# YOCO decoder trunk: the first mixer's input products of two chunks by Strassen's scheme, and half of the gained weights split at first use

## The chip, the cores and the metric

The kernel runs on one core of a Trainium2 chip. The metric is the device time of one execution in microseconds (us); lower is better. Three runs of the kernel before took 1886.28, 1886.26 and 1881.32 us, so its median is 1886.26 us.

## The reference, cut to what matters

One sequence of 2048 positions, width 1024, 8 heads of 64, everything in fp32:

```python
h = rmsnorm(x, norm_a)
b, c, xin, g = split(h @ w_in_a, 4)             # (2048 x 1024) @ (1024 x 4096)
y = b * causal_conv3(c * xin, conv_a)           # depthwise, along the positions
x = x + (y * silu(g)) @ w_out_a
k, v = split(rmsnorm(x, norm_kv) @ w_kv, 2)     # computed once
h = rmsnorm(x, norm_b)
q, g = split(h @ w_in_b, 2)
o = stick_breaking_attention(q, k, v)           # strictly causal, no softmax
x = x + (o * silu(g)) @ w_out_b
out = rmsnorm(x, norm_f)
```

The change concerns `h @ w_in_a` for half of the positions, and the way in which `w_kv` and `w_in_b`, times their gains, are made ready for the later products.

## The kernel before

**Tiles.** Positions lie in 4 chunks of 512 columns; chunk 0 holds the last ones. The width is 8 blocks of 128 partitions. A product in fp32 is made from rounded halves: every operand is split into a high part (a cast on ScalarE, ACT) and a low part (a subtraction on VectorE, DVE; `split`, L174), and `mm3` (L203) runs high·high, high·low and low·high for each of the 8 contraction blocks: 24 matmuls of 128x512 into one PSUM bank, a "group". TensorE is PE below, GpSimd POOL, SyncE SP.

**The first mixer.** `mixer_in((0, 1))` (L284) is called m01 here. It runs over 8 channel blocks `cb`, the two chunks `c` and the four gates C, X, B, G: 64 groups. x of the two chunks is loaded once; it is multiplied by the gain `norm_a` only and split to `h` (L238, L239), so that products can start before the mean square of a position is known. Its reciprocal root, broadcast over partitions (`rs`, and `rs2`, its square, L250), is multiplied into the gates' results later (L331, L348, L350). The weights of each gate and block are loaded raw, split (`load_w`, L184) and stored split to DRAM for the chunks 2 and 3, which load them split.

**Beside it.** `stats_x` (L260) computes the mean squares of chunks 2 and 3, and `fold_gains` (L359) makes 16 blocks of w_kv and w_in_b ready: load in two halves, multiply by the gain (L368), split, store.

**Order.** The generators yield amounts of PE work, and `merge`, `take` and `run` interleave them by weights (L729 to L751): first a quarter of m01 alone, then the rest of it beside `stats_x` and `fold_gains`. After it come the out-projection of chunk 0 (`proj_out`, L376; `yr` is the mixer's y read back, `po` its product) and its k, q, v, then attention of the chunks, merged with the projections of others. The order on each engine is fixed when the program is built. An engine runs its instructions strictly in order, and SP starts nearly all DMAs, also in order, each after the semaphores that it waits for.

**Homes.** Tiles share named sets of buffers: a tile gets its buffer when the last reader of the tile that had it is done. m01's banks are `lin`, `z` and `wt`, two of each, in turn. Split weights are `whl`, 4 buffers of 8 KB a partition, raw ones `wraw`, 2 buffers. x lies in `w`, `R` and `ld`, the folds and `x1` in `og`.

## Time and profile before

| | us | share of the span |
|---|---|---|
| median of three runs | 1886.26 | |
| the profiled execution | 1879.31 | |
| its span, first to last instruction | 1877.6 | 100% |
| PE busy | 1771.9 | 94% |
| DVE busy | 1261.9 | 67% |
| ACT busy | 772.7 | 41% |
| POOL busy | 450.4 | 24% |
| the 16 DMA engines, on average, by the queue that SP and others feed | | 63.0% |

1.7 us of the profiled execution lie outside of its span, and it is 6.95 us shorter than the median. A busy PE is one that has a matmul in its pipeline; the granted clock, a share of full speed, says how fast it runs, and averages 0.979. The chain of waits is the work that ended last, followed back step by step to what released it; an instruction's idle time is the time that its engine stood still ahead of it, and the arrow after it names what ended that.

### The profile page before, as it was taken

The page shows a single profiled execution, that of the slowest core. Times are in us where ns is not written, and L with a number is a line of the kernel's source. Part 1 is how long each engine was busy: PE and PEld are TensorE (multiplying, and loading weights), DVE is VectorE, ACT ScalarE, POOL GpSimd, SP SyncE. Part 2 cuts the span into 40 slices and gives each one's busy share as a digit, 9 for nine tenths or more (in the row PEclk, how much of TensorE's full clock was granted, in tenths as well). Part 3 has the DMA queues.
Part 4 walks back from the last instruction along what each step waited for, and adds up shares of the span by engine and source line. Part 5 has one row for each costly group of instructions (what it writes and reads, how often), then busy time and mean ns, then how long its engine had stood idle before and what let it go on. Part 6 is the DMA issues. An engine that isn't in the chain of part 4 may idle for free.

```text
span 1877.6 us, 24951 instructions
## 1 busy us (share of the span) xinstructions
PE 1771.9 (94%) x8312; PEld 1447.6 (77%) x8312; DVE 1261.9 (67%) x1927; ACT 772.7 (41%) x1497; POOL 450.4 (24%) x822
## 2 busy tenths in 40 slices
PE   7999999999999999999999999999988998988783
PEld 5888888888778878887888888888766886866562
DVE  7876534554243364478785478787858889889984
ACT  6423212231232143345443244454535556556642
POOL 5100000101111032132221122232223214547543
PEclk9999999999999999999999999999999999999896
DMA  9999865697978798867677766566586667778763
GB/s 292 309 324 332 307 195 165 209 328 280 336 250 281 227 330 257 290 207 250 216 253 244 248 195 204 183 215 198 180 300 196 223 194 265 260 238 278 225 196 130
DMA packets 238480, 460.44 MB, mean 245 GB/s; under 512 B 18448, under 2 KB 133136, under 8 KB 213776
## 3 DMA queue, kind: packets, MB, share of 16 engines
q1 hardware_dynamic: 178272, 400.09, 63.0%
q10 hardware_dynamic: 59920, 58.74, 10.9%
q8 instruction: 66, 1.08, 0.2%
q14 instruction: 62, 0.51, 0.1%
q0 software_dynamic: 160, 0.02, 0.1%
HBM read 322.73 MB, written 136.05 MB: 244 GB/s over the span
## 4 chain that ended last, share of the span: by engine, by line
PE 74%; DVE 10%; DMA 7%; issue 4%; ACT 2%; POOL 2%; SPq 0%; ACTq 0%; POOLq 0%; DVEq 0%
PE pX L209 9%; PE pB L209 9%; PE po L209 9%; PE pG L209 9%; PE pC L209 8%; PE wt L526 4%; PE pv L209 4%; PE pk L209 3%; PE pq L209 3%; DVE R L514 3%; PE pg L209 3%; PE av L536 3%; PE av L535 2%; PE z L500 2%; PE z L501 2%
## 5 line engine op out<-in xcount | busy, mean ns | idle before, releaser
L514 DVE TENSOR_TENSOR_SCAN R<-R,R,ones 128x512 f32<-128x512 f32 x192 | 255.0, 1330 | 25.2 <-ACT R L503 24.7
L503 ACT ACTIVATE R<-z 128x512 f32<-128x512 f32 (+1 forms) x320 | 174.0, 544 | 185.0 <-PE z L501 72.7
L176 DVE TENSOR_TENSOR wtl<-wt,wth 128x512 fp32r<-128x512 f32 (+1 forms) x320 | 186.2, 601 | 79.9 <-ACT wth L175 76.8
L175 ACT CAST wth<-wt 128x512 fp32r<-128x512 f32 (+1 forms) x320 | 159.6, 528 | 184.7 <-PE wt L526 150.3
L518 DVE TENSOR_TENSOR w<-w,R 128x512 f32<-128x512 f32 (+1 forms) x320 | 207.7, 658 | 19.6 <-POOL R L511 2.1
L209 PE MATMUL pC<-h,whl_C 128*128 128x512 f32 x768 | 189.8, 396 | 11.0 <-ACT whl_C L175 8.0
L513 POOL COPY R<-R 128x1 f32<-128x1 f32 x192 | 117.4, 613 | 340.9 <-DVE R L514 308.6
L209 PE MATMUL po<-y,whl_o 128*128 128x512 f32 x768 | 189.2, 393 | 2.4 <-DVE x L394 2.0
L209 PE MATMUL pX<-h,whl_X 128*128 128x512 f32 x768 | 186.3, 392 | 1.3 <-DVE cv L354 1.3
L209 PE MATMUL pB<-h,whl_B 128*128 128x512 f32 x768 | 185.9, 392 | 0.0
L209 PE MATMUL pG<-h,whl_G 128*128 128x512 f32 x768 | 185.7, 392 | 0.0
L526 PE MATMUL wt<-ident,w 128*128 128x128 f32 x1088 | 176.8, 278 | 7.5 <-DVE w L518 4.5
L209 PEld LDWEIGHTS pC<-h,whl_C 128*128 128x128 f32 x768 | 143.5, 189 | 44.1 <-ACT whl_C L175 8.0
L505 ACT ACTIVATE w<-z 128x512 f32<-128x512 f32 (+1 forms) x320 | 172.1, 543 | 2.5 <-PE wt L526 2.4
L209 PEld LDWEIGHTS pX<-h,whl_X 128*128 128x128 f32 x768 | 143.5, 188 | 31.5 <-DVE cv L354 1.5
L209 PEld LDWEIGHTS po<-y,whl_o 128*128 128x128 f32 x768 | 142.7, 188 | 32.1 <-DVE x L394 2.2
L209 PEld LDWEIGHTS pB<-h,whl_B 128*128 128x128 f32 x768 | 143.5, 188 | 29.7
L209 PEld LDWEIGHTS pG<-h,whl_G 128*128 128x128 f32 x768 | 143.6, 188 | 29.5
L526 PEld LDWEIGHTS wt<-ident,w 128*128 128x128 f32 x1088 | 137.4, 143 | 36.0 <-DVE w L518 6.9
L536 PE MATMUL av<-wtl,vv 128*128 128x512 f32 (+1 forms) x320 | 127.3, 401 | 27.0 <-DVE wtl L176 26.5
L514 DVE TENSOR_TENSOR_SCAN R<-R,ones 128x512 f32<-128x512 f32 (+3 forms) x128 | 116.4, 915 | 37.0 <-POOL R L509 32.8
L500 PE MATMUL z<-kt,q 128*128 128x512 f32 (+1 forms) x320 | 129.3, 406 | 5.7 <-ACT w L505 2.8
(172 smaller groups left out, 2685.1 us busy)
## 6 DMA issues: line engine op xcount, KB each, us to landing
whl_o<-sw_o SPq DMA_DIRECT2D x24, 1024.0 KB, 5.3
kt<-k_d ACTq DMA_DIRECT2D x80, 256.0 KB, 4.0
vv<-v_d ACTq DMA_DIRECT2D x80, 256.0 KB, 3.7
whl_C<-sw_C SPq DMA_DIRECT2D x16, 1024.0 KB, 5.9
whl_X<-sw_X SPq DMA_DIRECT2D x16, 1024.0 KB, 5.3
whl_B<-sw_B SPq DMA_DIRECT2D x16, 1024.0 KB, 5.8
whl_G<-sw_G SPq DMA_DIRECT2D x16, 1024.0 KB, 5.3
whl_k<-sw_kv SPq DMA_DIRECT2D x16, 1024.0 KB, 7.0
```

Source lines behind the costliest of these rows:

```text
L175: nc.scalar.copy(hi, src)
L176: eng.tensor_sub(lo, src, hi.bitcast(F32))
L209: ins = nc.tensor.matmul(ps, w[:, k, :], a[k][:, m, :], start=n == 0, stop=n == 3 * kt - 1)
L500: nc.tensor.matmul(ps[:, lom:CH], q2[:, 0, qi * P:(qi + 1) * P], kt[:, lom:CH], start=True, stop=False)
L501: nc.tensor.matmul(ps[:, lom:CH], q2[:, 1, qi * P:(qi + 1) * P], kt[:, lom:CH], start=False, stop=True)
L503: nc.scalar.activation(R[:, lo + 1:CH + 1], ps[:, lo:CH], AF.Sigmoid, scale=-0.125)
L505: nc.scalar.activation(w[:, lo:CH], ps[:, lo:CH], AF.Sigmoid, scale=0.125)
L513: nc.gpsimd.tensor_copy(R[:, 0:1], carry[qi])
L514: nc.vector.tensor_tensor_scan(out=R[:, lo + 1:CH + 1], data0=R[:, lo + 1:CH + 1], data1=ones[:, 0:1].to_broadcast([P, CH - lo]), initial= ...
L518: nc.vector.tensor_mul(w[:, lo:CH], w[:, lo:CH], R[:, lo:CH])
L526: nc.tensor.transpose(wt[:, qi * P:(qi + 1) * P], ws[qi][:, kb * P:(kb + 1) * P], ident)
L536: ins = nc.tensor.matmul(av[:, 0:n], vs, wl[:, 0:n], start=False, stop=final)
```

## The change

**Strassen's scheme.** For channel blocks 2 to 7 of m01 two gates (C and X, or B and G) and the two chunks form a 2x2 block product over the two halves of the contraction (k blocks 0 to 3 and 4 to 7): rows are the gates, columns the chunks. Winograd's form needs 7 products of half length in place of 8. Such a unit has 7 x 4 x 3 = 84 matmuls in place of 96, and there are 12 units. The operands are sums. On the weights' side, for every unit (`fast_weights`): a11, a21, a22, a12 and s1 to s4, from 4 raw tiles, 8 splits, two DVE and two POOL additions. On the x side, once (`fast_operands`, called at the second channel block, and `fast_rest`, at the start of the fast part): x of both chunks is scaled by gain and reciprocal root in 16 DVE instructions, 16 POOL subtractions make the sums, and 28 tiles are split: b11, t1, t2, b22, b21, t3, t4, 4 tiles each. The results are put together by `keep` (ACT copies out of PSUM, 4 a unit) and 3 DVE additions. Since x is scaled, the multiplications by `rs` and `rs2` go there.

**First use.** `fold_gains` makes 8 of its 16 blocks in m01. The other 8 (k and q blocks 2 and 3, g blocks 0 to 3) are loaded raw, multiplied and split by `load_w` where they are first used, in `proj_rest(0)` and in the gate projection of chunk 2.

**Halves.** Split weights are held, loaded and stored in halves of 4 k blocks (256 and 512 KB a DMA in place of 512 and 1024), everywhere.

**Smaller edits.** The gate of the two chunks uses Silu in place of Sigmoid and a product; x and the bank of sums have other homes; loads of `stats_x` and `fold_gains` are held behind PE's progress (`follow`); chunk 0's last y stays in SBUF (`y_last`); the weights of `merge` and `take` change.

```diff
-NR, NW, NT, NL, NWB, NRAW, NA, NWTS = 5, 8, 4, 5, 4, 2, 16, 2
+NR, NW, NT, NL, NWB, NRAW, NA, NWTS = 5, 8, 4, 5, 8, 4, 16, 2
...
+NPL = 2
+Q = 4
...
+    def load_w(src, key, nm, kt=KD, eng=nc.vector, gain=None):
+        first = key not in split_d
+        if first:
             split_d[key] = dram.tile([P, 2, kt, P], F32, name=f"sw_{nm}")
-            nc.sync.dma_start(out=split_d[key], in_=wt.bitcast(F32))
-            return wt
-        wt = w_tile(nm, kt)
-        nc.sync.dma_start(out=wt.bitcast(F32), in_=split_d[key])
-        return wt
+        wts = []
+        for j in range(0, kt, Q):
+            wt = w_tile(f"{nm}_{j}")
+            if first:
+                raw = sb.tile([P, Q, P], F32, name=f"wr_{nm}_{j}", tag="wraw", bufs=NRAW)
+                nc.sync.dma_start(out=raw, in_=src[j * P:(j + Q) * P, :].rearrange("(k p) n -> p k n", p=P))
+                if gain is not None:
+                    nc.vector.tensor_mul(raw, raw, gain[:, j:j + Q].unsqueeze(2).to_broadcast([P, Q, P]))
+                split(wt[:, 0], wt[:, 1], raw, eng)
+                nc.sync.dma_start(out=split_d[key][:, :, j:j + Q, :], in_=wt.bitcast(F32))
+            else:
+                nc.sync.dma_start(out=wt.bitcast(F32), in_=split_d[key][:, :, j:j + Q, :])
+            wts.append(wt)
+        return wts
...
-            tag, bufs = (("w", NW), ("R", NR) if k < NR else ("ld", NL))[c]
+            tag, bufs = (("og", KD), ("ld", NL) if k < NL else ("vv", 2) if k == NL else ("ot", 2))[c]
...
+            x = sb.tile([P, CH], F32, name=f"xs_{c}_{k}", tag="og", bufs=KD)
+            follow(nc.sync.dma_start(out=x, in_=xT[k * P:(k + 1) * P, cols(c)]))
...
-        for cb in range(KD):
+        for cb in range(KD if len(cs) == 1 else NPL):
             wts = {}
+            if cb == NPL - 1 and len(cs) > 1:
+                fast_operands()
...
-                    nc.scalar.activation(sg, sg, AF.Sigmoid)
-                    nc.vector.tensor_mul(t, t, late[c][1])
+                    nc.scalar.activation(sg, sg, AF.Silu)
+                    nc.vector.tensor_mul(t, t, late[c][0])
                 else:
                     nc.scalar.activation(sg, pG, AF.Sigmoid)
                 nc.vector.tensor_mul(t, t, sg)
-                nc.vector.tensor_mul(t, t, pG)
+                if c not in late:
+                    nc.vector.tensor_mul(t, t, pG)
                 nc.sync.dma_start(out=y_d[c][cb], in_=t)
                 yield rest(24)
...
+        if len(cs) > 1:
+            yield from mixer_fast()
...
+    def fast_operands():
+        x0, x1 = x_in[1], x_in[0]
+        for k in range(Q):
+            for c, x in ((1, x0), (0, x1)):
+                nc.vector.scalar_tensor_tensor(out=x[k], in0=x[k], scalar=gains["a"][:, k:k + 1], in1=late[c][0],
+                                               op0=ALU.mult, op1=ALU.mult)
+        w2 = ("w", NW)
+        operand("b11", x0[:Q], [(w2, w2)] * Q)
+        for k in range(Q):
+            nc.gpsimd.tensor_sub(x0[k], x1[k], x0[k])
+        hs = [("R", NR)] * 5 + [("wth", NWTS)] * 2 + [("wtl", NWTS)]
+        operand("t1", x0[:Q], [(hs[2 * k], hs[2 * k + 1]) for k in range(Q)])
+        for k in range(Q):
+            for c, x in ((0, x1), (1, x0)):
+                nc.vector.scalar_tensor_tensor(out=x[k + Q], in0=x[k + Q], scalar=gains["a"][:, k + Q:k + Q + 1],
+                                               in1=late[c][0], op0=ALU.mult, op1=ALU.mult)
+            nc.gpsimd.tensor_sub(x0[k], x1[k + Q], x0[k])
+            nc.gpsimd.tensor_sub(x1[k], x1[k + Q], x1[k])
+    def fast_rest():
+        x0, x1 = x_in[1], x_in[0]
+        act = ["act"] * Q
+        operand("t2", x0[:Q], act)
+        operand("b22", x1[Q:], act)
+        operand("b21", x0[Q:], act)
+        operand("t3", x1[:Q], act)
+        for k in range(Q):
+            nc.gpsimd.tensor_sub(x0[k + Q], x0[k + Q], x0[k])
+        operand("t4", x0[Q:], ["q2", "q2", (("kt", 2), ("kt", 2)), (("vv", 2), ("vv", 2))])
+    def fast_weights(n, cb, gs):
+        nm = f"{gs[0][0]}{cb}"
+        if n % 2 == 0:
+            raws = [sb.tile([P, Q, P], F32, name=f"fr_{nm}_{i}", tag="wraw", bufs=NRAW) for i in range(4)]
+        else:
+            pair = sb.tile([P, 2, Q, P], F32, name=f"fr_{nm}", tag="hl", bufs=1)
+            raws = [pair[:, 0], pair[:, 1]] + [sb.tile([P, Q, P], F32, name=f"fr_{nm}_{i}", tag="ot", bufs=2) for i in range(2)]
+        a11, a12, a21, a22 = raws
+        w = {}
+        def sp(key, raw):
+            w[key] = w_tile(f"{key}_{nm}")
+            split(w[key][:, 0], w[key][:, 1], raw)
+        for key, raw, (g, i), j in (("a11", a11, gs[0], 0), ("a21", a21, gs[1], 0), ("a22", a22, gs[1], Q), ("a12", a12, gs[0], Q)):
+            src = w_in_a[0][j * P:(j + Q) * P, i * D + cb * P: i * D + (cb + 1) * P]
+            nc.sync.dma_start(out=raw, in_=src.rearrange("(k p) n -> p k n", p=P))
+        for key, raw, (g, i), j in (("a11", a11, gs[0], 0), ("a21", a21, gs[1], 0), ("a22", a22, gs[1], Q), ("a12", a12, gs[0], Q)):
+            sp(key, raw)
+            if (g, cb) not in split_d:
+                split_d[g, cb] = dram.tile([P, 2, KD, P], F32, name=f"sw_{g}{cb}")
+            nc.sync.dma_start(out=split_d[g, cb][:, :, j:j + Q, :], in_=w[key].bitcast(F32))
+            if key == "a22":
+                nc.vector.tensor_add(a22, a21, a22)
+                sp("s1", a22)
+                nc.gpsimd.tensor_sub(a21, a11, a21)
+                nc.vector.tensor_sub(a11, a22, a11)
+                sp("s2", a11)
+        nc.gpsimd.tensor_sub(a12, a12, a11)
+        sp("s4", a12)
+        sp("s3", a21)
+        return w
...
+        def product(bank, w, b, start, stop):
+            n = 0
+            for k in range(Q):
+                for i, m in ((0, 0), (0, 1), (1, 0)):
+                    beat[:] = [nc.tensor.matmul(bank, w[:, i, k, :], ops[b][k][m], start=start and n == 0,
+                                                stop=stop and n == 3 * Q - 1, skip_group_check=True)]
+                    n += 1
+            return 3 * Q * MM
...
+        def keep(nm, ps):
+            t = ld512(nm)
+            nc.scalar.copy(t, ps)
+            return t
...
+        def out_of(cb, c, b, g):
+            t = conv[cb, c]
+            nc.vector.tensor_mul(t, t, b)
+            sg = t512(f"sg_{cb}_{c}")
+            nc.scalar.activation(sg, g, AF.Silu)
+            nc.vector.tensor_mul(t, t, sg)
+            if c == 0 and cb == KD - 1:
+                y_last.append(act_tile("y_0", cb))
+                split(y_last[0][:, 0, :], y_last[0][:, 1, :], t)
+            else:
+                nc.sync.dma_start(out=y_d[c][cb], in_=t)
...
+        for n, (cb, gs) in enumerate(units):
+            nm = f"{gs[0][0]}{cb}"
+            w = ws.pop(n)
+            a = bank(f"fa_{nm}", "lin", NLIN)
+            d = bank(f"fd_{nm}", "z", NZ)
+            c = bank(f"fc_{nm}", "wt", NWT)
+            yield product(a, w["a11"], "b11", True, False)
+            c0 = keep(f"f1_{nm}", a)
+            yield product(d, w["s1"], "t1", True, False)
+            p5 = keep(f"f5_{nm}", d)
+            final = n == len(units) - 1
+            if not final:
+                ws[n + 1] = fast_weights(n + 1, *units[n + 1])
+            if prev:
+                yield last_product(n - 1)
+            yield product(a, w["s2"], "t2", False, False)
+            c1 = keep(f"f2_{nm}", a)
+            yield product(d, w["s4"], "b22", False, True)
+            nc.vector.tensor_add(c1, c1, d)
+            if not final:
+                yield product(c, w["a12"], "b21", True, True)
+                nc.vector.tensor_add(c0, c0, c)
+            yield product(a, w["s3"], "t3", False, False)
+            x1 = keep(f"f3_{nm}", a)
+            nc.vector.tensor_add(x1, x1, p5)
+            if final:
+                yield product(c, w["a12"], "b21", True, True)
+                nc.vector.tensor_add(c0, c0, c)
+            if n % 2 == 0:
+                conv[cb] = conv_of(cb, 0, x1, c1)
+            else:
+                out_of(cb, 0, c1, x1)
+            prev.append((cb, gs, w, a, c0, c1, x1))
+        yield last_product(len(units) - 1)
...
+    def fold_gains(blocks):
...
+    def load_kv(i, nm):
+        return load_w(w_kv[:, i * P:(i + 1) * P], ("kv", i), nm, gain=gains["kv"])
...
+            if c == 0 and k == KD - 1:
+                y.append(y_last[0])
+                continue
             y.append(act_tile(f"y_{c}", k))
-            t = ld512(f"yr_{c}_{k}")
+            t = sb.tile([P, CH], F32, name=f"yr_{c}_{k}", tag="og", bufs=KD) if c == 0 else ld512(f"yr_{c}_{k}")
...
-        wts = load_w(None, ("kv", kb), f"k{c}_{kb}")
+        wts = load_kv(kb, f"k{c}_{kb}")
...
-    run(take(m01, TA / 4))
-    merge((m01, 1.75 * TA), (chain(iter((DLY,)), stats_x(2), stats_x(3), fold_gains()), 18.0 + DLY))
+    run(take(m01, TA / 2))
+    merge((m01, 1.3 * TA), (chain(iter((DLY,)), stats_x(2), stats_x(3), fold_gains([("kv", 0), ("b", 0), ("kv", 4), ("kv", 1), ("b", 1), ("kv", 5), ("kv", 6), ("kv", 7)])), 10.0 + DLY))
```

The rows below give the order on an engine in the program: line, operation, tile written, tiles read. A name ends in block, chunk and a running number, which differs between the two programs.

First DVE, where the fast part begins. `op_` tiles are the x side's operands (their raws are `xh_chunk_block`), `whl_` the weight side's, of unit C2 (block 2, gates C and X) and B2 (B and G); `sg` and `cv` are the end of the block before, of the old scheme.

```order
L177 TENSOR_TENSOR op_b21_3_1128<-xh_1_7_560,op_b21_3_1128 128x512
L177 TENSOR_TENSOR whl_s3_C2_1200<-fr_C2_2_1163,whl_s3_C2_1200 128x512
L177 TENSOR_TENSOR op_t3_0_1131<-xh_0_0_251,op_t3_0_1131 128x512
L177 TENSOR_TENSOR op_t4_0_1147<-xh_1_4_545,op_t4_0_1147 128x512
L369 TENSOR_TENSOR sg_1_1_1089<-pG_1_1_1064,rs_1_704 128x512
L177 TENSOR_TENSOR op_t3_1_1134<-xh_0_1_269,op_t3_1_1134 128x512
L177 TENSOR_TENSOR op_t3_2_1137<-xh_0_2_274,op_t3_2_1137 128x512
L177 TENSOR_TENSOR op_t4_1_1150<-xh_1_5_550,op_t4_1_1150 128x512
L177 TENSOR_TENSOR op_t3_3_1140<-xh_0_3_279,op_t3_3_1140 128x512
L177 TENSOR_TENSOR whl_a11_B2_1241<-fr_B2_1234,whl_a11_B2_1241 128x512
L177 TENSOR_TENSOR op_t4_2_1_1154<-xh_1_6_555,op_t4_2_0_1153 128x512
L374 TENSOR_TENSOR cv_1_1_1059<-cv_1_1_1059,sg_1_1_1089 128x512
```

Before, the same place of the program reads so; `whl_G2` is a full block of weights, `fold1_kv4` a fold.

```order
L348 TENSOR_TENSOR sg_1_1_984<-pG_1_1_959,rs_1_681 128x512
L368 TENSOR_TENSOR fold1_kv4_4_1753<-fold1_kv4_4_1753,g_kv_77 128x512
L176 TENSOR_TENSOR whl_G2_0_1217<-wr_G2_0_1218,whl_G2_0_1217 128x1024
L353 TENSOR_TENSOR cv_1_1_954<-cv_1_1_954,sg_1_1_984 128x512
L176 TENSOR_TENSOR fold1_kv4_4_1753<-fold1_kv4_4_1753,fold0_kv4_4_1752 128x512
L354 TENSOR_TENSOR cv_1_1_954<-cv_1_1_954,pG_1_1_959 128x512
```

The instruction that reads the last bank of the old scheme (`sg_1_1`) now stands behind the b21 splits and among those of t3 and t4, where folds and a weight stood.

PE at the start of the fast part, in the program of the change: `fc_C2` is the third product of the first unit, `fa_B2` the first of the second unit, `fa_C2` goes on with the first unit.

```order
L483 MATMUL fc_C2_1205<-op_b21_0_1119,whl_a12_C2_1192 128x512 x3
L483 MATMUL fc_C2_1205<-op_b21_1_1122,whl_a12_C2_1192 128x512 x3
L483 MATMUL fc_C2_1205<-op_b21_2_1125,whl_a12_C2_1192 128x512 x3
L483 MATMUL fc_C2_1205<-op_b21_3_1128,whl_a12_C2_1192 128x512 x3
L483 MATMUL fa_B2_1332<-op_b11_0_0_755,whl_a11_B2_1241 128x512
L483 MATMUL fa_B2_1332<-op_b11_0_1_756,whl_a11_B2_1241 128x512
L483 MATMUL fa_C2_1203<-op_t2_0_1095,whl_s2_C2_1189 128x512 x3
```

Before, that place holds the eight rows of `pC_2_0`, x3 each, that follow `pG_1_1`; their operands had been ready since the first block. Two matmuls of the second unit now stand ahead of the first unit's t2 product; `fa_B2` takes a `lin` bank.

ACT at the end of m01, in the program of the change: `y_0` are the casts that make chunk 0's y ready for `proj_out`, `sg_7_1` the gate from the last product of m01 (`fa_B7`).

```order
L493 COPY f3_B7_3207<-fa_B7_3094 128x512
L176 CAST whl_o0_2_4_3443<-wr_o0_2_4_3444 128x512
L176 CAST whl_o0_3_0_3482<-wr_o0_3_0_3483 128x512
L518 ACTIVATE sg_7_0_3224<-f3_B7_3207 128x512
L518 ACTIVATE sg_7_1_3243<-fa_B7_3094 128x512
L176 CAST whl_o0_3_4_3488<-wr_o0_3_4_3489 128x512
L176 CAST y_0_7_3227<-cv_7_0_3158 128x512
L176 CAST y_0_0_3247<-yr_0_0_3248 128x512
L176 CAST y_0_1_3252<-yr_0_1_3253 128x512
```

Before, on ACT at the end of m01:

```order
L175 CAST y_0_5_3002<-yr_0_5_3003 128x512
L175 CAST y_0_6_3007<-yr_0_6_3008 128x512
L349 ACTIVATE sg_7_0_2834<-sg_7_0_2834 128x512
L318 COPY cs_7_1_2866<-pC_7_1_2841 128x512
L175 CAST whl_o0_0_3018<-wr_o0_0_3019 128x1024
L175 CAST y_0_7_3012<-yr_0_7_3013 128x512
```

Seven of the eight y casts stood ahead of the gate of the last block; all of them now stand behind `sg_7_1`.

More of the change, by code (lines that the diff above doesn't have):

```diff
@@ L203, in mm3 @@
     def mm3(ps, wts, a, kt=KD):
-        hi, lo = wts[:, 0], wts[:, 1]
         n = 0
         for k in range(kt):
-            for w, m in ((hi, 0), (hi, 1), (lo, 0)):
-                ins = nc.tensor.matmul(ps, w[:, k, :], a[k][:, m, :], start=n == 0, stop=n == 3 * kt - 1)
+            for w, m in ((0, 0), (0, 1), (1, 0)):
+                ins = nc.tensor.matmul(ps, wts[k // Q][:, w, k % Q, :], a[k][:, m, :], start=n == 0, stop=n == 3 * kt - 1)
                 if fine[1] and len(anchors) > SLACK and n % GRP == 0:
@@ L281 @@
     turn = [0]
-    late_acc, late = {}, {}
+    late_acc, late, x_in = {}, {}, {}
     def mixer_in(cs):
@@ new lines, in fold_gains @@
+    def fold_gains(blocks):
+        for nm, i in blocks:
+            src, gain = (w_kv, gains["kv"]) if nm == "kv" else (w_in_b[0], gains["b"])
+            split_d[nm, i] = dram.tile([P, 2, KD, P], F32, name=f"sw_{nm}{i}")
+            for j in range(0, KD, Q):
+                hi, lo = (sb.tile([P, Q, P], F32R, name=f"fold{m}_{nm}{i}_{j}", tag="og", bufs=KD) for m in range(2))
+                raw = lo.bitcast(F32)
+                follow(nc.sync.dma_start(out=raw, in_=src[j * P:(j + Q) * P, i * P:(i + 1) * P].rearrange("(k p) n -> p k n", p=P)))
+                nc.vector.tensor_mul(raw, raw, gain[:, j:j + Q].unsqueeze(2).to_broadcast([P, Q, P]))
+                split(hi, lo, raw)
+                for m, t in enumerate((hi, lo)):
+                    nc.sync.dma_start(out=split_d[nm, i][:, m, j:j + Q, :], in_=t.bitcast(F32))
+            yield 1.0
```

102 lines of the change are left out of this document (70 added, 32 removed).

## Prediction

> **What bounds the kernel now.** I read the table of stages first (busy time of each engine, its count of instructions, granted clock, share of the DMA engines, GB/s). The second and third row below are the part in which m01 runs with full order.
>
> ```profile
> core 0: us, PE busy (x) PEld busy (x) DVE busy (x) ACT busy (x) POOL busy (x), PEclk, DMA share, GB/s
> 62.20:106.20 44.00, 44.00 (x195) 36.45 (x194) 30.67 (x46) 15.73 (x24) 2.46 (x5) 1.00 0.88 305
> 106.20:369.30 263.10, 263.10 (x1170) 218.28 (x1169) 141.05 (x212) 65.72 (x91) 12.80 (x27) 1.00 0.75 250
> 369.30:560.00 190.70, 185.60 (x831) 152.55 (x830) 82.22 (x145) 48.38 (x91) 19.24 (x49) 0.98 0.86 298
> 1000.00:1400.00 400.00, 394.05 (x1929) 325.28 (x1927) 291.26 (x422) 181.98 (x374) 97.48 (x201) 0.99 0.65 217
> ```
>
> Between 106.2 and 369.3 PE is never idle, at full clock, and DVE is busy for 141.05 of 263.10 us (54%). Nothing but the count of matmuls sets this stage. The chain of waits says the same of the whole, and PE's timeline (start, duration, and in brackets the idle time before) gives the price:
>
> ```profile
> PE 74%; DVE 10%; DMA 7%; issue 4%; ACT 2%; POOL 2%; SPq 0%; ACTq 0%; POOLq 0%; DVEq 0%
> 100.80 5.60 PE L209 MATMUL pG<-h,whl_G 128*128 128x512 f32 x24
> 106.23 5.60 PE L209 MATMUL pC<-h,whl_C 128*128 128x512 f32 x24
> 111.68 0.95 PE L127 MATMUL pst_h<-ones,acc_h 128*128 128x1 f32 x8
> 363.82 5.60 PE L209 MATMUL pG<-h,whl_G 128*128 128x512 f32 x24
> 369.26 5.61 PE L209 MATMUL po<-y,whl_o 128*128 128x512 f32 x24
> ```
>
> From start to start a group of 24 takes 5.44 us (363.82 to 369.26; 5.43 at 100.80), 0.2267 us a matmul. The 48 groups of blocks 2 to 7 (6 x 2 x 4) are 261.1 us, the statistics' sums two times 0.8 (111.68 to 112.48 by the next group), together the 263.
>
> **The change, part by part**, against the profiled execution's 1879.31 us, which is 6.95 below the median of 1886.26.
>
> *1. Fewer matmuls.* 12 units drop 12 matmuls each: 144 x 0.2267 = 6 x 5.44 = **-32.6 us**. The stage would be 228.5 us. All else is whether PE can be fed at this rate, for DVE, ACT and POOL now do in 228 us what they did not have to do in 263.
>
> *2. The way into the fast part.* Before, the operand `h` was there from the first block. Now 28 tiles of operands must be made between the moment at which the reciprocal root of chunk 1 is broadcast and the products that use them. That moment and the prices of DVE:
>
> ```profile
> 67.20 0.69 DVE L331 TENSOR_TENSOR p<-p,rs 128x512 f32<-128x512 f32 x1 [1.91 <-ACT rs L255]
> 47.24 0.69 DVE L176 TENSOR_TENSOR fold_kv<-fold_kv,fold_kv 128x512 fp32r<-128x512 f32 x1
> 47.84 0.69 DVE L172 TENSOR_TENSOR acc_h<-acc_h,sq_h 128x512 f32<-128x512 f32 x1
> 48.44 0.75 DVE L339 SCALAR_TENSOR_TENSOR cv<-p,cw,cv 128x512 f32<-128x512 f32 x1
> 49.10 0.69 DVE L172 TENSOR_TENSOR acc_h<-acc_h,sq_h 128x512 f32<-128x512 f32 x1
> L175 ACT CAST fold_kv<-fold_kv 128x512 fp32r<-128x512 f32 x16 | 9.9, 621 | 32.8 <-DVE fold_kv L368 32.8
> fold_kv<-in_w_kv_dram SPq DMA_DIRECT2D x16, 256.0 KB, 6.2
> ```
>
> A subtraction follows the next after 0.60 us (47.24 to 47.84), a scaling after 0.66 (48.44 to 49.10). POOL has a price for DVE too. In the first stage it adds squares while DVE scales:
>
> ```profile
> 26.07 8.75 POOL L172 TENSOR_TENSOR acc_h<-acc_h,sq_h 128x512 f32<-128x512 f32 x5 [0.27 <-ACT sq_h L171]
> 29.09 2.89 DVE L239 SCALAR_TENSOR_TENSOR h<-xh,g_a,h 128x512 fp32r<-128x512 f32 x2
> 9.08 0.75 DVE L239 SCALAR_TENSOR_TENSOR h<-xh,g_a,h 128x512 fp32r<-128x512 f32 x1
> 28.49 0.68 DVE L325 TENSOR_TENSOR p<-pX,cs 128x512 f32<-128x512 f32 x1
> 11.55 1.28 POOL L172 TENSOR_TENSOR acc_h<-acc_h,sq_h 128x512 f32<-128x512 f32 x1 [0.59 <-ACT sq_h L171]
> ```
>
> Five POOL additions take 1.75 us each there and two DVE scalings 2.89, in place of 0.75 for one alone; the DVE product that reads PSUM (0.68) is not slowed. I charge every POOL subtraction of two SBUF tiles 1.75 - 0.66 = 1.1 us of DVE's time, if DVE has such work just then; zero is the other bound. The Trainium skill ("SBUF — State Buffer", section "SBUF: two separate sides") speaks against this change: it has DVE and GpSimd share a port pair that one of them locks for a whole instruction. The trace agrees in kind; by the rule an operation would cost DVE its 1.28 us alone, an estimate some 3 us longer at this place than the sum below.
>
> By the order, DVE has 58 instructions from 66.7 (the scale is ready) to the last b21 split: 14 scalings x 0.66 + 44 others x 0.60 = 35.7 us, with 14 POOL subtractions x 1.1 = 15.4 more: 117.8. PE comes to b21 (third product) at 106.23 + 24 x 0.2267 = 111.7 and could end it at 114.4; its last three matmuls need the last of the four tiles, so it ends near 118.1: **+3.7**. Next on PE stands `fa_B2`, whose `lin` bank comes free with `sg_1_1`: four more DVE rows and two subtractions (4.6 us) put that at 122.4: **+4.3**. Eight DVE rows (4.8) later, at 127.2, the last t4 split frees the `ot` buffers for unit B2's raw a21 and a22; load 6.2, then cast, split, addition, cast, split (2.8): s1 of B2 is ready at 136.3. PE has four more products (48 x 0.2267 = 10.9) and stands at 133.3: **+3.0**. In sum **+11** (0 if POOL holds up nothing, since DVE is then done with b21 at 102.4 and PE asks at 111.7; 16 if eight more DVE instructions, 5 us, of the blocks before fall into this stretch).
>
> *3. The clock.* PE's idle time lowers it:
>
> ```profile
> 505.99 5.77 PE L209 MATMUL pv<-xn,whl_v 128*128 128x512 f32 x24 [1.34 <-DVE khl L176]
> 518.76 8.44 PE L209 MATMUL pv<-xn,whl_v 128*128 128x512 f32 x24 [1.62 <-DVE qhl L176]
> 518.00:524.00 6.00, 5.24 (x12) 4.15 (x13) 4.48 (x10) 0.58 (x1) 0.94 (x4) 0.50 0.51 178
> ```
>
> A group after a thin stretch took 8.44 in place of 5.60 us, at a granted 0.50: 2.8 us lost. Another, after an idle time of 1.34, lost 0.2. Three waits of 3 to 4 us: **+2** (0 to 5). The Trainium skill ("TensorE: Matmul & The Clock Gate", section "HAM oscillation — how this bites in real kernels") has the clock fall after idle gaps of more than about 3.4 us; here it fell behind several gaps of 0.5 to 1.6 us, so the row is stricter. By the rule two of the three waits would count, some 5 us as an estimate, the upper end.
>
> *4. The way out.* Before, PE went from the last pG to po with no gap, since ACT had cast most of chunk 0's y by then (five of them here):
>
> ```profile
> 342.94 3.34 ACT L175 CAST y<-yr 128x512 fp32r<-128x512 f32 x5 [3.81 <-PE pG L209]
> 41.17 0.87 DVE L157 TENSOR_SCALAR dg_h<-ident,yl_h 128x128 fp32r<-128x128 f32 x4
> ```
>
> That is 26 us ahead of po at 369.26, at 0.67 us each. Now all eight stand behind `sg_7_1` (order above), which waits for the last product, and po waits for y_0_0. On that path lie, after the last product, a DVE product (0.6), eight of the small scalings of the second row (1.6; they stand there by the order), the gate (0.6), the cast of a weight (0.6), y_0_7 and y_0_0 with its subtraction (0.6 each): some 4.7 us, of which the four matmuls that still stand there hide 0.9: **+4** (2 to 8: the four ACT instructions alone, 4 x 0.52 by the group above, or all eight casts at 0.67 and four more of these instructions).
>
> *5. Steady units.* A unit lasts 84 x 0.2267 = 19.04 us. DVE has in it on average 18 instructions (8 splits, 2 additions of weights, 3 of results, 5 of the conv and gate, by the order) x 0.61 = 11.0, two POOL subtractions x 1.1 = 2.2, and 46 instructions of statistics and folds over the 12 units (2.4): 15.6 of 19.04, 82%. That fits, but what is late by 2 us in a unit is no longer hidden by 21.8 us of matmuls: **+2** (0 to 10).
>
> *6. Later stages.* Eight blocks are now folded at their first use: 4 DVE instructions x 0.60 = 2.4 us and 2 casts each, in chunk 0's projections (DVE 43% busy in 369 to 560) and near 1300 (73%). Weight loads come in rows of 2 KB in place of 8 KB; DMA share is 0.65 to 0.86 there. The first use takes its load of 6.2 us ahead, since the loads are issued as the buffers come free. And the order of attention is shuffled, by some rows to either side. No row prices that; the nearest are PE's idle times, 5.1 us in 369 to 560 and 6 in 1000 to 1400. -4 is most of the first taken back, by a better order; +10 is half of 8 x 2.4 on the path. PE is 97 to 99% busy there, so that DVE has cover, and I take a value near the hidden end: **+2** (-4 to +10).
>
> *7. Start.* PE's rows are unchanged up to 106.2 and PE has no idle time between 62.2 and 106.2: **0**. The third table load of ACT and one DVE product less a group cancel below 1 us.
>
> Sum: -32.6 + 11 + 2 + 4 + 2 + 2 = -11.6, 1867.7 us in terms of the profiled execution, with 6.95 for the median **1875 us**.
>
> **Rivals.** A, the way in is hidden: POOL doesn't hold DVE up, or the scheduler's slack covers it. For it: without POOL it is 35.7 us of work in the 45 from 66.7 to 111.7. Against it: the 2.89 us row. Terms 2 and 3 fall: 1875 - 13 = **1862**. B, slower: DVE becomes the bound of the fast part. POOL's subtractions and casts that come late stretch DVE's 15.6 us beyond 19.04. At 20.5 us a unit, 12 x 1.5 = 18 us are lost on top: **1893**. It turns slower than before by 0.3% at 20.4 us a unit ((1892 - 1875) / 12 + 19.04). Against it: 82% on average; for it: block 4, which by the order holds the statistics of chunks 2 and 3, is denser, and a unit's chain of raw, a22, s1, s2, s4 is serial over three engines. C, the gain is given back later: the eight first uses and the new order of attention cost their upper bound, about 9 us more than term 6: **1884**. That PE would keep its 96 matmuls a unit is excluded: the order shows 84.
>
> **How the numbers follow.** Chances: forecast 0.50 (gain 6 to 20 us), A 0.20, C 0.18, B 0.12. About 0.3% (5.7 us, 1880.6 to 1891.9) is what a measurement of this kernel can tell from no change. Forecast and A are faster: 0.70; C within: 0.18; B slower: 0.12. The range holds forecast, A's lower side (1862 less 4 of term 6) and C: 1857 to 1891, which leaves out B and A's far end.
>
> **What would show it.** po would start near 356 (369.26 - 32.6 + 19) in place of 369.26 in PE's timeline. The waits of PE would be released by `op_b21`, by `sg`, and by `whl_s1_B2`, between 112 and 137, with POOL's subtractions near 1.75 us and DVE's splits above 0.7 beside them, and the granted clock below 1.00. Ahead of po an idle time of 4 us would end with ACT's or DVE's y. A chain without these waits makes A right; PE idle ahead of most units, with DVE near 100%, makes B right; po at 356 but an end later than 1868 makes C right. A loss ahead of 106.2 would make the whole forecast wrong, since I hold that part unchanged.

## The result and the profile after

The changed kernel takes 1909.51 us in the median of 4 runs (1903.29 to 1910.81), the kernel before 1884.47 with one more run. The ratio is 1.0128, 95% interval 1.0100 to 1.0156: **slower by 25 us**, where some 11 us less were forecast. The profiled execution took 1903.29 us (span 1901.6); it is the shortest of the four, 6.2 us below their median.

The table of stages of the changed kernel, cut where its own stages end (columns as in the table of before):

```profile
core 0: us, PE busy (x) PEld busy (x) DVE busy (x) ACT busy (x) POOL busy (x), PEclk, DMA share, GB/s
62.20:106.20 44.00, 44.00 (x196) 36.40 (x195) 39.59 (x47) 16.68 (x29) 25.63 (x17) 1.00 0.27 92
106.20:377.10 270.90, 248.47 (x1031) 197.93 (x1029) 199.88 (x315) 122.94 (x221) 54.57 (x54) 0.94 0.72 233
377.10:560.00 182.90, 173.64 (x770) 142.35 (x771) 91.16 (x156) 50.57 (x94) 19.52 (x45) 0.97 0.95 314
1000.00:1400.00 400.00, 390.30 (x1918) 322.26 (x1917) 297.43 (x433) 186.16 (x387) 92.81 (x210) 1.00 0.69 219
```

The second row ran from 106.2 to 369.3 before, with PE busy all the time. It holds 144 matmuls fewer and is nevertheless 7.8 us longer: PE stands still for 22.4 us, and the clock is 0.94. In the third row the DMA share has gone from 0.86 to 0.95. PE's waits from 106 to 385, by what ended them (us in total, times, longest):

```profile
PE fa_B L483 <- ACT f_B L493: 7.4, 2, 6.9
PE fa_B L483 <- DVE sg L369: 3.8, 1, 3.8
PE fc_C L483 <- DVE op_b L177: 2.3, 1, 2.3
PE po L217 <- ACT y L176: 2.2, 1, 2.2
PE fa_C L483 <- DVE p L500: 2.2, 1, 2.2
PE pst_h L130 <- DVE acc_h L173: 2.1, 1, 2.1
```

And PE's timeline at the two ends of the fast part:

```profile
107.51 2.96 PE L483 MATMUL fa_C<-op_b,whl_a_C 128*128 128x512 f32 x12
...
117.23 1.44 PE L483 MATMUL fc_C<-op_b,whl_a_C 128*128 128x512 f32 x5 [2.33 <-DVE op_b L177]
122.49 1.19 PE L483 MATMUL fa_B<-op_b,whl_a_B 128*128 128x512 f32 x2 [3.82 <-DVE sg L369]
124.05 5.46 PE L483 MATMUL fa_C<-op_t,whl_s_C 128*128 128x512 f32 x12 [0.37 <-ACT f_C L493]
129.34 2.91 PE L483 MATMUL fd_C<-op_b,whl_s_C 128*128 128x512 f32 x12
132.09 2.49 PE L483 MATMUL fa_B<-op_b,whl_a_B 128*128 128x512 f32 x10
...
362.15 0.39 PE L483 MATMUL fc_B<-op_b,whl_a_B 128*128 128x512 f32 x1
369.40 5.49 PE L483 MATMUL fa_B<-op_t,whl_a_B 128*128 128x512 f32 x12 [6.87 <-ACT f_B L493]
377.12 0.73 PE L217 MATMUL po<-y,whl_o 128*128 128x512 f32 x2 [2.23 <-ACT y L176]
```

With 0.2267 us a matmul this gives an account of the profiled execution against the one before:

| stretch | how | us |
|---|---|---|
| matmuls left out | 144 x 0.2267 | -32.6 |
| ahead of the fast part | 107.51 against 106.23 | +1.3 |
| way in, 107.51 to 132.09 | 24.6 for 62 matmuls (14.1) | +10.5 |
| units, 132.09 to 362.38 | 230.3 for 934 matmuls and two sums of statistics (213.3) | +17.0 |
| way out, 362.38 to po at 377.12 | 14.7 for 12 matmuls (2.7) | +12.0 |
| from po's start to some 430 | see below | +5.5 |
| behind that | the rest of 24.0 between the spans | +10.6 |

The last two rows compare the two kernels where PE has the same amount left to do (columns of its matmuls, summed from the end of the timeline): the changed one is 13.4 us late where the one before is at 424, 7.9 at po and 24.0 at the end. The rows add up to 0.3 more than that, since their prices are rounded.

The 17.0 us of the units can be added up matmul by matmul. Eight matmuls that PE waited for began 8.1 us late in sum (PE's idle time is 6.8 of that). The 32 matmuls that ran slow without a wait, most of them behind the two longest waits at a granted clock of 0.50, cost 5.5. The other 893 took 0.2298 us each in place of 0.2267, 2.8 in sum. The remaining 0.6 lie around the statistics' sums.

Why PE waits 6.87 us ahead of the last product is in ACT's timeline and, for its cause, in that of SP's queue (start, duration, instruction):

```profile
357.36 0.62 ACT L176 CAST whl_o<-wr_o 128x512 fp32r<-128x512 f32 x1
368.24 0.62 ACT L176 CAST whl_o<-wr_o 128x512 fp32r<-128x512 f32 x1 [10.26 <-DMA wr_o<-in_w_out_a_dram]
368.77 0.58 ACT L493 COPY f_B<-fa_B 128x512 f32<-128x512 f32 x1
369.25 1.26 ACT L176 CAST whl_o<-wr_o 128x512 fp32r<-128x512 f32 x2
370.41 0.62 ACT L518 ACTIVATE sg<-f_B 128x512 f32<-128x512 f32 x1
374.92 0.60 ACT L518 ACTIVATE sg<-fa_B 128x512 f32<-128x512 f32 x1 [3.88 <-PE fa_B L483]
```

```profile
354.76 3.35 SPq L607 DMA_DIRECT2D yr<-y_d  x4
358.15 1.18 SPq L201 DMA_DIRECT2D sw_o<-whl_o  x2
359.43 1.18 SPq L618 DMA_DIRECT2D x<-in_xT_dram  x1
360.66 1.22 SPq L201 DMA_DIRECT2D sw_o<-whl_o  x1
361.92 2.94 SPq L197 DMA_DIRECT2D wr_o<-in_w_out_a_dram  x3
```

The bank of the last product (`fa_B7`) may only be added to again when ACT has copied it (`f3_B7`). That copy stands on ACT behind the cast of a weight of the out-projection, whose raw load left SP only at 361.92, behind loads of y, stores and a load of x; the cast could begin 6.3 us later. A copy that could run at 362.4 ran at 368.8.

The longest wait among the units has the same form, with one engine more between. These rows are of ACT, DVE and PE, in this order:

```profile
189.37 0.63 ACT L172 ACTIVATE sq_h<-xs 128x512 f32<-128x512 f32 x1 [2.06 <-DMA xs<-in_xT_dram]
189.91 0.60 ACT L176 CAST whl_a_C<-fr_C 128x512 fp32r<-128x512 f32 x1
190.54 0.69 DVE L177 TENSOR_TENSOR whl_a_C<-fr_C,whl_a_C 128x512 fp32r<-128x512 f32 x1 [1.78 <-ACT whl_a_C L176]
192.35 0.69 DVE L500 TENSOR_TENSOR p<-fa_C,f_C 128x512 f32<-128x512 f32 x1
193.09 4.14 PE L483 MATMUL fa_C<-op_b,whl_a_C 128*128 128x512 f32 x11 [2.23 <-DVE p L500]
```

ACT waits 2.06 us for a load of x for the statistics (`sq_h` are its squares); behind that square stands the cast of a weight, behind the cast on DVE its split, and behind that the product `p`, which frees PE's bank. PE had written this bank's last product by 185.4.

Behind po's start, where the account has +5.5, PE waits again, 2.01 us for DVE's `dg_hb`, a row of the statistics, and 0.90 for a y, and then runs 94 matmuls in 23.1 us, from start to start, in place of 21.3:

```profile
380.09 0.80 PE L161 MATMUL prb_hb<-dg_hb,onesr 128*128 128x512 f32 x1 [2.01 <-DVE dg_hb L160]
381.78 23.26 PE L217 MATMUL po<-y,whl_o 128*128 128x512 f32 x94 [0.90 <-DVE y L177]
```

### The profile page after: what moved, and what is told of

It is laid out like the page before. It is cut to its first block, busy times and chain, and to the rows that moved or that the text cites. A ratio compares the mean times of both kernels' runs of the same rounds, so it can differ in the third digit from the quotient of the medians.

```text
span 1901.6 us, 25430 instructions
## 1 busy us (share of the span) xinstructions
PE 1765.7 (93%) x8168; PEld 1431.0 (75%) x8168; DVE 1350.9 (71%) x2067; ACT 835.7 (44%) x1650; POOL 498.8 (26%) x862
## 3 DMA queue, kind: packets, MB, share of 16 engines
q1 hardware_dynamic: 250816, 391.19, 63.1%
## 4 chain that ended last, share of the span: by engine, by line
PE 55%; DVE 10%; DMA 7%; issue 4%; POOL 2%; ACT 1%; SPq 0%; ACTq 0%; POOLq 0%; DVEq 0%
PE po L217 8%; PE pC L217 4%; PE pv L217 4%; PE pG L217 4%; PE pX L217 4%; PE wt L751 4%; PE pk L217 4%; PE pq L217 4%; PE pB L217 4%; DVE R L739 3%; PE pg L217 3%; PE av L761 2%; PE z L725 2%; PE av L760 2%; PE z L726 2%
## 5 line engine op out<-in xcount | busy, mean ns | idle before, releaser
L738 POOL COPY R<-R 128x1 f32<-128x1 f32 x192 | 109.3, 570 | 366.9 <-DVE R L739 332.4
L751 PEld LDWEIGHTS wt<-ident,w 128*128 128x128 f32 x1088 | 138.8, 143 | 39.4 <-DVE w L743 12.1
L725 PE MATMUL z<-kt,q 128*128 128x512 f32 (+1 forms) x320 | 129.5, 407 | 8.3 <-ACT w L730 7.2
L734 POOL TENSOR_SCALAR_AFFINE_SELECT R<-R 128x128 f32<-128x128 f32 x128 | 56.0, 438 | 298.3 <-ACT R L728 272.4
L217 PE MATMUL pC<-h,whl_C 128*128 128x512 f32 x480 | 124.1, 403 | 10.4 <-ACT whl_C L176 6.9
L760 PE MATMUL av<-wth,vv 128*128 128x512 f32 (+1 forms) x320 | 122.4, 383 | 8.1 <-ACT wth L176 6.5
L726 PE MATMUL z<-kt,q 128*128 128x512 f32 (+1 forms) x320 | 120.1, 378 | 0.0
L217 PE MATMUL pG<-h,whl_G 128*128 128x512 f32 x480 | 118.4, 392 | 1.1 <-DVE whl_G L177 0.9
L217 PE MATMUL pX<-h,whl_X 128*128 128x512 f32 x480 | 118.8, 392 | 0.3 <-ACT whl_X L176 0.3
L217 PE MATMUL pB<-h,whl_B 128*128 128x512 f32 x480 | 118.3, 392 | 0.0
L217 PEld LDWEIGHTS pC<-h,whl_C 128*128 128x128 f32 x480 | 90.5, 192 | 33.4 <-ACT whl_C L176 6.9
```

The costliest lines, as they stand in the source:

```text
L217: ins = nc.tensor.matmul(ps, wts[k // Q][:, w, k % Q, :], a[k][:, m, :], start=n == 0, stop=n == 3 * kt - 1)
L725: nc.tensor.matmul(ps[:, lom:CH], q2[:, 0, qi * P:(qi + 1) * P], kt[:, lom:CH], start=True, stop=False)
L726: nc.tensor.matmul(ps[:, lom:CH], q2[:, 1, qi * P:(qi + 1) * P], kt[:, lom:CH], start=False, stop=True)
L751: nc.tensor.transpose(wt[:, qi * P:(qi + 1) * P], ws[qi][:, kb * P:(kb + 1) * P], ident)
L760: nc.tensor.matmul(av[:, 0:n], vs, wh[:, 0:n], start=first, stop=False)
```

## The experiments

Each was timed in 3 or 5 rounds beside the kernel before, and a difference is to its median in the same series (1883.45 for 1 to 4, 1884.45 for 5 to 7 and the first of 8, 1882.63 for the rest); the changed kernel stands at +25.0 (its interval is 19 to 29). "po" is the start of the out-projection in PE's timeline (before 369.26, changed 377.12).

**1. Old products, the other edits kept.** `NPL = 8`, so that all blocks go by the old scheme and nothing of the fast part is built (the calls of the fast part are guarded accordingly).

```diff
-NPL = 2
+NPL = 8
```

> The changed kernel with the 48 groups of channel blocks 2 to 7 by the old scheme again (24 matmuls a group); first use, halves, homes and Silu as changed. Theory: the fast part lost its whole gain on itself and at its two ends, and the other edits cost some 11 us after the out-projection of chunk 0. Then PE has no idle time between 107 and po, po starts at 369 to 372 (changed kernel: 377.1, before: 369.3), and the whole is 8 to 14 us slower than before. Rival: the other edits cost nothing, all of the loss hangs on the fast part: within 4 us of before.

1892.64 us (+9.2), ratio 1.0060 (1.0039 to 1.0081); po at 370.13, no idle time of PE between 106 and po. So some 9 us are lost without Strassen's scheme, and nearly all of them behind po.

**2. The subtractions on DVE.**

```diff
-            nc.gpsimd.tensor_sub(x0[k], x1[k], x0[k])
+            nc.vector.tensor_sub(x0[k], x1[k], x0[k])
```
(likewise the other three lines of x-side subtractions)

> The 16 subtractions of the x side's operands on DVE in place of POOL. Theory: each POOL subtraction held DVE for 1.1 us, more than the 0.60 that DVE needs to do it itself, so the last b21 split comes about 7 us earlier (near 110 to 111), PE's waits for it and for sg (2.3 and 3.8 us) fall below 1 us together, the slow product behind them goes, and a new wait of 0 to 3 us for s1 of the second unit shows; PE is 7 to 10 us earlier by 140. Rival: it is the count of DVE instructions, POOL overlaps anyway: 16 more instructions on DVE make both waits longer, by up to 9 us in sum.

1896.08 us (+12.6), ratio 1.0072 (1.0046 to 1.0098), 12.4 better than the changed kernel; po at 366.24, 10.9 earlier. The positions are of the profiled execution, which was the slowest of the seven (1906.15 us), so the 10.9 us at po and the 12.4 of the medians are not of one execution. At the way in PE now waits so:

```profile
122.29 0.73 PE L483 MATMUL fa_C<-op_t,whl_s_C 128*128 128x512 f32 x2 [0.79 <-ACT f_C L493]
...
134.25 2.12 PE L483 MATMUL fd_B<-op_t,whl_s_B 128*128 128x512 f32 x8 [1.08 <-DVE whl_s_B L177]
```

The waits for b21 and sg are gone, a short one for s1 of the second unit shows, as expected. The way in takes 15.8 us in place of 24.6, and the units 226.7 in place of 230.3. With sixteen more instructions DVE is ready sooner. In the changed kernel the rows of DVE and POOL that stand beside each other (DVE from 79, POOL from 80) show why:

```profile
79.19 1.78 DVE L362 SCALAR_TENSOR_TENSOR cv<-p,cw,cv 128x512 f32<-128x512 f32 x1
80.89 1.78 DVE L177 TENSOR_TENSOR op_t<-xh,op_t 128x512 fp32r<-128x512 f32 x1
82.59 1.78 DVE L352 TENSOR_TENSOR p<-p,rs 128x512 f32<-128x512 f32 x1
86.00 0.68 DVE L364 TENSOR_TENSOR cv<-cv,pB 128x512 f32<-128x512 f32 x1
```

```profile
80.38 1.74 POOL L428 TENSOR_TENSOR xh<-xh,xh 128x512 f32<-128x512 f32 x1
82.08 1.74 POOL L419 TENSOR_TENSOR xh<-xh,xh 128x512 f32<-128x512 f32 x1
```

The two engines step in turn, at 1.70 us for one instruction of each (79.19, 80.89, 82.59), where DVE alone does one in 0.60. Of these rows only the product that reads a bank (`pB`) is not held up.

**3. The weights' casts behind the copy.** The casts of the out-projection's weights of chunk 0 get an ordering edge: block 1 behind the last product, block n behind the first matmul of block n-2's group.

```diff
-        nc.scalar.copy(hi, src)
+        cast = nc.scalar.copy(hi, src)
+        if after is not None:
+            tc.add_manual_dep(cast.ins, after.ins.name, PACE, reason="pace")
```

> The casts of the out-projection's weights of chunk 0, block 1 on, stand behind the last product of the fast part on ACT, and block n behind the first matmul of block n-1 less one, so that no copy out of PSUM, gate or y cast stands behind a cast that waits for a raw load. Theory: PE's wait of 6.9 us ahead of the last product goes (below 1 us), the 2.8 us of slow clock with it, and po starts at 367 to 369 in place of 377.1; the whole gains 6 to 10 us. Rival: y itself is late, since its loads share the DMA engines with the same raw loads: the wait moves to po, which starts at 373 or later.

1901.38 us (+17.9), ratio 1.0097 (1.0063 to 1.0131), 7.1 better than the changed kernel, though the two intervals overlap; po at 368.44, 8.7 earlier:

```profile
363.68 3.05 PE L487 MATMUL fa_B<-op_t,whl_a_B 128*128 128x512 f32 x12 [0.45 <-ACT f_B L497]
368.44 0.77 PE L219 MATMUL po<-y,whl_o 128*128 128x512 f32 x2 [1.71 <-ACT y L176]
```

The wait of 6.87 us falls to 0.45 and the last product's 5.49 to 3.05, so it was ACT's order that made the wait; the rival, a late y, would have moved it to po, which waits 1.71 here and 2.23 in the changed kernel. What the expectation says of "block n-1 less one" is the edge named above.

**4. All folds in the first mixer.** `fold_gains` makes its 16 blocks again, with weight 18 in `merge`.

> All 16 gained blocks are folded inside the first mixer again (weight 18 in the merge), none at first use. Theory: the eight first uses cost 5 to 6 us around 1280 to 1360, which comes back, but 48 more DVE instructions and 24 more DMAs of 256 KB net fall into the fast part, whose DVE is 75 to 80% busy: po starts 3 to 10 us later than 377; the whole is within 6 us of the changed kernel. Rival: first use costs nothing, then the whole is slower than the changed kernel by what po loses.

1909.36 us (+25.9), ratio 1.0136 (1.0103 to 1.0169); po at 381.56. Of the 4.4 us that po loses 3.1 are back where PE has as much left as the kernel before at 424, and the medians agree. First use does show in PE's timelines. Between the points where the kernel before is at 1200 and at 1300 the changed kernel falls 3.2 us further behind, this one 0.3; by 1400 1.1 us of the difference are left. So it holds about 1 us by this reading, and is not where the time went.

**5. Both ends.** Experiments 2 and 3 together.

> The subtractions on DVE and the late casts together. If the way in and the way out are independent losses, po starts near 357 to 358 (377.1 less 10.9 and 8.7 that the two edits gave alone), and the whole is near 1888 (1909.5 less 13.4 and 8.1), still 2 to 8 us above before, because the part behind the out-projection keeps its 8 to 13 us. Rival: the two ends share one cause (PE runs into the same late DMAs sooner), then the second edit adds less than 4 us.

1888.56 us (+4.1), ratio 1.0019 (1.0004 to 1.0033); po at 355.54. The losses add: 21.6 us at po where the edits gave 10.9 and 8.7, and 20.9 in all where they gave 12.4 and 7.1. The kernel is still not faster than before, with PE 13.7 us ahead at po. In the profiled execution some 6 us are lost by the point where the kernel before is at 424, 9 more by 1540 and 10 near 1550, of which experiment 8 tells.

**6. Old products, all folds in the first mixer.** Experiments 1 and 4 together: of the change, halves, homes, Silu, `follow` and the merge weights are left.

> Old products for all blocks and all 16 gained blocks folded in the first mixer: of the change only halves, homes, Silu and the merge weights are left. Theory A: first use makes the 9 us by which the old products with the other edits are slower than before; then this comes within 3 us of before. Theory B: halves (rows of 2 KB, more DMAs) or the order that follows from them make it; then this stays 5 to 10 us above before.

1896.51 us (+12.1), ratio 1.0063 (1.0043 to 1.0084); po at 370.50. That is theory B, with more than its 5 to 10 us.

**7. The kernel before in halves.** Only weights in halves of 4 blocks, as in the change.

> The kernel before with weights held, loaded and stored in halves of 4 blocks, and nothing else changed. Theory B (halves cost it): 4 to 10 us slower than before, most of it behind 1250. Theory A (first use costs it): within 3 us of before.

1897.06 us (+12.6), ratio 1.0062 (1.0041 to 1.0083). Halves alone cost 12.6 us.

**8. Rows of 4 KB.** A half of the split weights is one block in DRAM, 4 KB for each partition; a half used to be two rows of 2 KB for each, cut out of an 8 KB block. PE, DVE, ACT and POOL have exactly the same order; on SP only the shapes differ, of stores as of loads.

```diff
-            split_d[key] = dram.tile([P, 2, kt, P], F32, name=f"sw_{nm}")
+            split_d[key] = dram.tile([kt // Q, P, 2, Q, P], F32, name=f"sw_{nm}")
...
-                nc.sync.dma_start(out=wt.bitcast(F32), in_=split_d[key][:, :, j:j + Q, :])
+                nc.sync.dma_start(out=wt.bitcast(F32), in_=split_d[key][j // Q])
```

Put on three kernels. With both ends mended:

> Both ends mended, and each half of the split weights stored in DRAM as one block with 4 KB for a partition in place of two rows of 2 KB. If the number of packets costs time (DMA queue of SP 250816 packets in place of 178272), the part behind the out-projection gains 3 to 8 us against the kernel with both ends mended. Rival: the DMA engines have room there (share 0.67 to 0.86), then within 2 us.

1875.01 us (-9.4), ratio **0.9945** (0.9928 to 0.9963): 13.5 better, where 3 to 8 were expected. On the changed kernel with no other edit:

> The changed kernel with nothing but the 4 KB rows; order on PE, DVE and ACT unchanged. Theory: the same 9 to 14 us as behind the mended ends, 1896 to 1901. Rival: with the ends unmended the loads have more time, and less than 6 us come.

1896.26 us (+13.6), ratio 1.0064 (1.0044 to 1.0085): 11.4 better. On the kernel before in halves:

> The kernel before in halves, with each half stored as one block of 4 KB a partition; order on PE, DVE and ACT as in the kernel before in halves. Theory: the 12.6 us that halves cost come from rows of 2 KB, not from the count of DMAs or from the new order; then 8 to 13 us come back and it is within 4 us of before. Rival: the new order or the doubled count of DMAs holds half of it or more: 6 us above before or more.

1888.74 us (+6.1), ratio 1.0032 (1.0015 to 1.0049): 6.5 of the 12.6 us come back, 6.1 stay. That is the rival's bound: about half of what halves cost is the rows, half something else. The intervals of the two kernels overlap (1.0041 to 1.0083 and 1.0015 to 1.0049), so the half is a rough one. The table of DMA issues (KB each, median us to landing) shows the price of a row; the first line is of the kernel with both ends mended, the second of the same with 4 KB rows, the third of the kernel before, with 8 KB rows:

```profile
whl_o<-sw_o SPq DMA_DIRECT2D x48, 512.0 KB, 5.3
```

```profile
whl_o<-sw_o SPq DMA_DIRECT2D x48, 512.0 KB, 4.4
```

```profile
whl_o<-sw_o SPq DMA_DIRECT2D x24, 1024.0 KB, 5.3
```

In these rows half a block in rows of 2 KB lands as late as a whole one in rows of 8 KB, and there are two halves to a group. SP is held longer too: it took 0.52 us to issue a load of split weights in rows of 2 KB and 0.32 in rows of 4 KB (medians of 320, both ends mended). Which of the two delays PE, the landing or SP's turn, no run separates.

The other half of what halves cost sits at one place. Between 940 and 900 matmuls' worth of columns left, the kernel in halves with 4 KB rows falls from 1.2 to 8.8 us behind, and every kernel built with halves loses 7.5 to 10 us there. PE's timeline of that kernel:

```profile
1550.93 0.50 PE L539 MATMUL av<-wth,vv 128*128 128x512 f32 x1 [1.23 <-ACT wth L176]
1552.98 0.59 PE L504 MATMUL z<-kt,q 128*128 128x512 f32 x1 [1.55 <-ACT w L509]
...
1555.69 0.80 PE L540 MATMUL av<-wtl,vv 128*128 128x512 f32 x1 [1.69 <-DVE wtl L177]
```

and of the kernel before, where a projection's matmuls fill this stretch, and no wait shows:

```profile
1549.19 4.37 PE L209 MATMUL pg<-xa,whl_gg 128*128 128x512 f32 x18
1553.39 0.39 PE L535 MATMUL av<-wth,vv 128*128 128x512 f32 x1
```

So attention's steps stand back to back where a group of the projection stood between them. That this order makes the loss is read from the two timelines; no experiment mended it.

**9. Early y.** On the mended kernel with 4 KB rows, chunk 0's y is read back and split beside the last unit, where `t2` and `b22` free their buffers.

```diff
+            if final:
+                y_early.extend(read_y(0))
...
-        y = []
+        y = read_y(c) if c else y_early + y_last
```

> Both ends mended, 4 KB rows, and chunk 0's y read back and split beside the last unit, so that its casts stand ahead of the last gate on ACT. Theory: what is left of the way out is the chain last product, gate, cast of y, po and the start of po at the pace of the casts; po starts 1 to 3 us earlier (352 to 354) and loses 2 to 4 us less behind its start: 1869 to 1873. Rival: only the last y, which hangs on the last product, sets it: within 2 us of the kernel with both ends mended and 4 KB rows (1875).

1869.45 us (-13.2), ratio **0.9927** (0.9902 to 0.9952), the fastest of all, 3.8 better than the kernel with both ends mended and 4 KB rows. The intervals of the two overlap; in their timelines PE is 3.9 us further ahead where the kernel before is at 370, and 5.3 at 424. PE's timeline:

```profile
346.58 2.88 PE L487 MATMUL fa_B<-op_t,whl_s_B 128*128 128x512 f32 x12
349.30 4.92 PE L219 MATMUL po<-y,whl_o 128*128 128x512 f32 x21
354.06 2.96 PE L487 MATMUL fa_B<-op_t,whl_a_B 128*128 128x512 f32 x12
```

21 of the first 24 matmuls of po need only the seven y that are read back; they now run ahead of the last product and cover its wait for ACT. Po itself starts at 349.30, ahead of the 352 to 354 expected, since the expectation had all of it behind the last product.

## Why the prediction was wrong

The direction was wrong and the time outside of the range. Steps 4, 5 and 6 were too low by 13.5, 15.0 and 8.6 us; the steps ahead of them held. No rival had the time either; the slowest, B, stood at 1893.

*1, fewer matmuls:* right. Undisturbed matmuls of the units run at nearly the old pace (0.2298 against 0.2267 us), and with the ends mended PE is 13.7 us ahead at po (experiment 5).

*2 and 3, the way in and the clock:* +13 forecast, +10.5 measured. The end of the b21 product was put at 118.1 and `sg` at 122.4; the product ended at 118.67, and PE went on with `fa_B` at 122.49. The mechanism (POOL holds DVE at about 1.1 us an instruction) is shown by experiment 2. The third wait, for s1 of the second unit, did not come: by then PE was late itself. The clock took 2.6 us (12 matmuls in 5.29 from start to start at 124.05, in place of 2.72). One instruction of each engine took 1.70 us, DVE's alone 0.60: 1.10 for a subtraction, the value taken. By the lock for a whole instruction of which the Trainium skill tells ("SBUF — State Buffer", section "SBUF: two separate sides"), the pair would take an estimated 0.60 + 1.28 = 1.88 us. The turns agree with it; the time is a tenth shorter.

*4, the way out:* **the first step that failed.** I priced the chain behind the last product at +4, at most 8 (the parts named there add up to 5.2, not 4.7; less the 0.9 that is hidden, it is still some 4). That chain was not the trouble. From the end of the last product at 374.89 to po at 377.12 it took 2.2 us, and with the casts moved the whole way out takes 5.4 us, 2.7 more than its 12 matmuls (experiment 3). In the changed kernel it was +12.0 ahead of po and +5.5 behind its start. I read ACT's order from `sg_7_1` on and did not ask what stands ahead of `f3_B7`, which the last product itself waits for: a cast whose raw load is late on SP, behind loads that the same way out issues. So a wait that the sum put at nothing cost 6.87 us, and the slow clock behind it 2.8. Experiment 3 takes 8.7 us of it at po: the order made the wait, not the work. Experiment 9 then takes a further 3.8 of the whole, a difference within the intervals.

*5, steady units:* **the step with the largest miss.** +2 forecast with an end at 10; +17.0 measured. I compared DVE's work with PE's time in a unit and left out that ACT and DVE stand still, in order, behind a load. The two longest waits, for `p` (2.2) and `acc_h` (2.1), both follow a load of x for the statistics: the rows above show it for `p`, and `acc_h` was added at 222.53, behind a square that began at 221.87 when its load had landed at 221.85, and took 1.75 us beside a POOL subtraction. Each was followed by matmuls at a granted clock of 0.50. A unit lasted 20.7 us on average, which is the size of rival B's loss, but not its cause: DVE was busy for 75% of the units' time, and PE waited eight times, not ahead of most units. Experiment 2 takes back 3.6 us here. No experiment took the loads or the statistics out of the units, and with both ends mended 11.4 of the 17.0 us stay.

*6, later stages:* +2 forecast, end at +10; +10.6 measured behind 424. Three parts of it can be told apart. The 2 KB rows, which I set at nothing since the DMA share was 0.65 to 0.86, cost 11.4 us of the changed kernel by the medians of experiment 8; the two profiled executions differ by 7.3 us, 3.3 of it ahead of the point where the kernel before is at 424, so that some 4 fall into this step. First use, the part to which I gave the price, holds about 1 (experiment 4). The place near 1550 takes 8.2, from 17.9 to 26.1 us behind, of which 2.4 are back soon after. Rival C had the sign, the place and nearly the size of this step (2 + 9); of its two causes first use is small, the new order of attention fits the place near 1550 but is not shown, and the rows it did not name.

*7, the start:* +1.3 where 0 was forecast. That is not the sign by which the whole forecast would be wrong: the start of the fast part lies between 107.05 and 109.71 in the eight kernels that have one, whose programs differ little ahead of it.

## What to carry to other kernels

When an engine is full and work is taken from it, the gain must survive every instruction that the engine now reaches earlier: at each end of the changed part, look at what stands ahead of the instruction that releases it, on that one's engine, and back to the queue that feeds that, not only at what stands behind. The same question belongs to the inside of that part, where a load for other work can hold up the engine. If a tile is cut in two, cut its copy in DRAM in the same way: rows of 2 KB in place of 4 KB cost 6.5, 11.4 and 13.5 us in three kernels, where the left-out matmuls were worth 32.6. And count a GpSimd addition of two SBUF tiles as DVE's own time, or more, if DVE then works on SBUF tiles: here 1.10 us against 0.60.

## What was unexpected of the hardware

512 KB of `whl_o` in rows of 2 KB landed in 5.3 us, in rows of 4 KB in 4.4, and 1024 KB in rows of 8 KB in 5.3. The share of the 16 DMA engines hardly showed it: 63.1% with 250816 packets in the changed kernel, 63.0% with 178272 before, and 62.1% with 201664 when 4 KB rows took 13.5 us off the kernel with both ends mended. That a copy in half as long pieces costs so much with the same order on PE, DVE, ACT and POOL could not be read from that share; what moved was the time to landing and SP's time to issue.
